# Two gate projections of group A moved from job 8 to the turn between groups B and A

## The chip, the cores and the metric

One core of one Trainium2 chip runs the whole program. The metric is device time in microseconds (us) of one launch, as the median of repeated runs. A core has five engines that run their own instruction streams in order and meet through semaphores: PE (TensorE, matmuls; its weight loads are listed as PEld), DVE (VectorE), ACT (ScalarE), POOL (GpSimd) and SP (SyncE, which here issues the DMAs).

## The reference, cut to what matters

One layer: `h = rms_norm(x)`, one projection of `h` (1024 tokens by 1024) onto 7,752 + 512 columns, four token mixers on slices of it, a SiLU gate on every mixer's output, one output projection and a residual.

```python
(aq, ak, av, ag, bq, bk, bv, bg, cq, ck, cv, cg, cf, d_in, dg) = _split(h @ w_in, IN_WIDTHS)
oa = rms_norm(differential_attention(rms_norm(aq), rms_norm(ak), av)) * (1 - lam_init)  # 4 heads
ob = rms_norm(stick_breaking_attention(bq, bk, bv))                                     # 8 heads
oc = rms_norm(forgetting_attention(rms_norm(cq), rms_norm(ck), cv, log_f))              # 8 heads
od = rwkv7_branch(d_in, ...)                                                            # 8 heads
mixed = concat([oa * silu(ag), ob * silu(bg), oc * silu(cg), od * silu(dg)])            # 2048 wide
out = x + mixed @ w_out
```

All gates are 16 blocks of 128 columns, numbered f = 0 to 15: 0 to 3 belong to A, 4 to 7 to B, 8 to 11 to C, 12 to 15 to D.

## The kernel before, in words

Everything is float32 in and out. A product is made of three fast matmuls on a high and a low part (`wh*hTh + wh*hTl + wl*hTh`), so one **projection** of 128 columns (`proj`, L271) is 2 halves of 512 tokens by 8 blocks of depth by 3 matmuls = 48 matmuls of 128x512, all on line L280, into two PSUM banks of the tag `pj`, of which there are only two. Its weights come in two pieces (`load_w`, L180): SP loads `raw` (256 KB, L186), ACT makes the high part `wh` (L191), POOL the low part `wl` (L192); each of these has two buffers, which one projection fills. After each half `evac` takes the bank out.

Order of work: the RWKV preparation of group D first; then 12 **jobs** (L1115), pairs of B heads (jobs 0 to 3), the A heads (4 to 7), pairs of C heads (8 to 11); then the RWKV chain, which begins once the normalised input and the weight buffers are given back after the last projection (`hp.close()`, L1150), and the output projection. In job i the program writes down the attention of job i, then the projections q, k, v of job i+1, then **fill**: the gate projections in `FILL[i]`. `FILL[8]` is gates 9, 0, 1. A planner turns this into one instruction order per engine: on its own estimate of time it takes on each engine the ready instruction that was written first. So fill and projections stand in the gaps of the attention that was written earlier, and buffers go to whoever was written earlier.

A gate is finished in one of two ways. Up to job 3 ACT's sigmoid table is loaded: `proj_gate` (L393) takes a sigmoid from the bank, multiplies on DVE, and stores 256 KB to `gates` in DRAM. From job 7 on the exp and ln tables are used: `proj_gate_exp` (L402) copies the bank to `gg` on ACT (L405), takes exp on ACT (L407), an add on DVE (L664), ln and exp on ACT (L665, L666), a multiply on POOL (L409), and stores (L410).

At the **turn** from B to A (job 3) the table is changed once (`exp_ln_tables`, L140/L141). The q and k of A's head 0 were projected before that and kept raw in DRAM (`late_qk`); after the table load they are loaded back (L365) and normalised half by half (`finish_qk`, L327: two squares on ACT, a difference on DVE, two `psn` matmuls, ln and exp on ACT, a product `qn` on DVE L339, then DMAs of line L133 that place q and k for the scores). The projections of A's head 1 follow.

After its attention every A head is stored raw (`otb`); `finish_later` loads it and its gate in a later job (`FIN`: gate 0 in job 8, gate 1 in job 9), normalises, multiplies and stores `mix`.

Tables of the file: `FILL` L45, `FIN` L46, `TMPB` L49 (buffers of the tag `tmp`), `HOLD` L55.

Of the kernel before, what the change touches and what calls it, by code (L numbers as in the profile page):

```python
# [10 lines left out]
F32 = mybir.dt.float32  # L11
# [3 lines left out]
AF = mybir.ActivationFunctionType  # L15
# [4 lines left out]
P = 128  # L20
S = 1024
DM = 1024
KT = DM // P
HS = 512
# [9 lines left out]
COL = dict(aq=0, ak=512, av=1024, ag=1536, bq=2048, bk=2560, bv=3072, bg=3584,  # L34
           cq=4096, ck=4608, cv=5120, cg=5632, cf=6144, dr=6152, dk=6664, dv=7176,
           dlo=7688, dg=7752)
# [6 lines left out]
EXP_LN_SET = 6  # L43
LATE_A = 4
FILL = {0: [4], 1: [5], 2: [6], 3: [7], 7: [8], 8: [9, 0, 1], 9: [10, 2], 10: [11, 3], 11: []}  # L45
FIN = {4: [4], 5: [5], 6: [6], 7: [7], 8: [0], 9: [1], 10: [2]}  # L46
OHW = 1152
NAV = 2
TMPB = 5  # L49
# [5 lines left out]
HOLD = (11,)  # L55
# [35 lines left out]
def hybrid_trunk_kernel(  # L91
# [23 lines left out]
    nc = tc.nc  # L115
# [3 lines left out]
    def pool(stack, name, bufs=1, space=None, side="left"):  # L119
        kw = {"side": side, "reuse_waits": "tile"} if space is None else {"space": space}  # L120
        return stack.enter_context(tc.tile_pool(name=name, bufs=bufs, **kw))

    dram = pool(ctx, "dram", 1, DRAM)
# [3 lines left out]
    def bank(tag, bufs, name):  # L127
        return psum.tile([P, HS], F32, tag=tag, bufs=bufs, name=name)
# [19 lines left out]
    def after(inst, first):  # L148
        tc.add_manual_dep(inst.ins, first.name if isinstance(first, mybir.InstLoadActFuncSet) else first.ins.name, mybir.DependencyInfo(
            mybir.DependencyClass.NoSync, mybir.DependencyReason.DATA), reason="order")  # L150
# [29 lines left out]
    def load_w(col, M=P, cols2=None):  # L180
        m1 = M if cols2 is None else M - cols2[1]
        wts = []
        for kh in range(2):
            rows = slice(kh * 4 * P, (kh + 1) * 4 * P)
            raw = wp.tile([P, 4, P], F32, tag="raw", bufs=2, name="raw")
            w_dma.append(nc.sync.dma_start(raw[:, :, :m1], w2[rows, col:col + m1].rearrange("(k p) c -> p k c", p=P)))  # L186
            if cols2 is not None:
                nc.sync.dma_start(raw[:, :, m1:M], w2[rows, cols2[0]:cols2[0] + cols2[1]].rearrange("(k p) c -> p k c", p=P))
            wh = wp.tile([P, 4, P], F32R, tag="wh", bufs=2, name="wh")
            wl = wp.tile([P, 4, P], F32R, tag="wl", bufs=2, name="wl")  # L190
            nc.scalar.copy(wh[:, :, :M], raw[:, :, :M])  # L191
            nc.gpsimd.tensor_sub(wl[:, :, :M], raw[:, :, :M], wh[:, :, :M].bitcast(F32))  # L192
            wts.append((wh, wl))
        return wts
# [48 lines left out]
    with xst:  # L243
# [14 lines left out]
        for hf in range(2):  # L258
            for kt in range(KT):
                ps = bank(("pj", "sc", "mm")[kt % 3] if hf == 0 else ("sc", "mm")[kt % 2], 2, "pst")  # L260
# [10 lines left out]
    def proj(col, evac, M=P, hold=None, wts=None):  # L271
        wts = load_w(col) if wts is None else wts
        pss = [bank("pj", 2, "pj") for _ in range(2)]
        for hf in range(2):
            cs = slice(hf * HS, (hf + 1) * HS)
            n = 0
            for kt in range(KT):
                wh, wl = wts[kt // 4]
                for a, b in ((wh, hTh), (wh, hTl), (wl, hTh)):
                    mm = nc.tensor.matmul(pss[hf][:M, :], lhsT=a[:, kt % 4, :M], rhs=b[:, kt, cs], start=n == 0, stop=n == 3 * KT - 1)  # L280
                    if n == 0 and hold is not None:
                        after(mm, hold)
                    n += 1
            evac(hf, cs, pss[hf])
# [5 lines left out]
    at = Att()  # L290
# [23 lines left out]
    def low_tiles(pl):  # L314
        at.units = 0
        at.low = [[], []]
        for h in range(2):
            other = slice(64 - 64 * h, 128 - 64 * h)
            for _ in range(3):
                t = pl.tile([P, HS], F32R, tag="ql", bufs=6, name=f"ql{h}")  # L320
                nc.gpsimd.memset(t[other].bitcast(F32), 0.0)
                at.low[h].append(t)
# [67 lines left out]
    gates = dram.tile([16, P, S], F32, name="gates")  # L390
    otb = dram.tile([8, P, S], F32, name="otb")

    def proj_gate(f, tmp):  # L393
# [5 lines left out]

        proj(COL["abcd"[f // 4] + "g"] + f % 4 * P, evac)  # L400

    def proj_gate_exp(f, hold=None):  # L402
        def evac(hf, cs, ps):
            g = at.cbp.tile([P, HS], F32, tag="gg", bufs=2, name="gg")
            nc.scalar.copy(g, ps)  # L405
            e = at.cbp.tile([P, HS], F32, tag="ge", bufs=2, name="gx")
            nc.scalar.activation(e, g, AF.Exp, scale=-1.0)  # L407
            sigmoid_of(e)
            nc.gpsimd.tensor_mul(e, g, e)  # L409
            nc.sync.dma_start(gates[f, :, cs], e)  # L410

        proj(COL["abcd"[f // 4] + "g"] + f % 4 * P, evac, hold=hold)

    def scores(t, h, qb, c0, c1, last=None):
        ps = bank("sc", 2, "sc")
# [247 lines left out]
    def sigmoid_of(e):  # L663
        nc.vector.tensor_scalar(e, e, 1e19, 1.0, op0=ALU.min, op1=ALU.add)  # L664
        nc.scalar.activation(e, e, AF.Ln)  # L665
        nc.scalar.activation(e, e, AF.Exp, scale=-1.0)  # L666
# [438 lines left out]
    with ExitStack() as st:  # L1105
        pl = pool(st, "attw", 1)
        low_tiles(pl)
        late_pools = st.enter_context(ExitStack())
        pp = pool(late_pools, "attp", 1)
        tmp = pool(late_pools, "attt", 1)  # L1110
        side = late_pools.enter_context(ExitStack())
        inv_load(pool(side, "ip", 1))
        bounds = INV_BOUNDS
        nxt = None
        for i, (pf, af, j) in enumerate(jobs):  # L1115
            cur = pf(j, pl, tmp) if nxt is None else nxt
            at.first = None
            af(j, cur, pl, pp, tmp)
            if i == 7:
                side.close()  # L1120
                at.cbp = pool(side, "cbp", 1)
            if i == 3:
                late = []
                nxt = proj_head_a(0, pl, tmp, late)
                for f in FILL[i]:
                    proj_gate(f, tmp)
                table = exp_ln_tables()
                for g in late:
                    g(table)
            else:  # L1130
                nxt = jobs[i + 1][0](jobs[i + 1][2], pl, tmp) if i + 1 < len(jobs) else None
            if i < 3:
                for f in FILL[i]:
                    proj_gate(f, tmp)
                gate_d(i, tmp)
                if i == 2:
                    gate_d(3, tmp)
            elif i >= 7:
                for f in FILL[i]:
                    proj_gate_exp(f, at.first if i in HOLD else None)  # L1140
            for f in FIN.get(i, []):
                for J in range(2):
                    finish_later(f, J, tmp)
            if i + 1 < len(bounds):
                with later(LATER):
                    inv_steps(bounds[i], bounds[i + 1], at.first)
                    if i + 2 == len(bounds):
                        inv_store()

        hp.close()  # L1150
        opr = pool(st, "opr", 1, side="right")
        rp = pool(st, "rp", 1, side="right")
        rwkv_chain_setup(rp)
        yts = {}

        def chain(c0, c1):
            for c in range(c0, c1):
                if c % 2 == 0:
                    yts[0] = rp.tile([P, 4, P], F32, tag="yt", bufs=2, name="yt")
                chunk_state(c, rp, yts[0], chunk_local(c + 1, rp) if c + 1 < NCH else iter(()))  # L1160
                if c % 2:
                    rwkv_norm(c // 2, yts[0], rp)

        for _ in chunk_local(0, rp):
            pass
        wo = {}
        chain(0, CUT1)
        split_w_early(pl, opr, wo)
        pair = out_blocks(0, 2, wo)
        for _ in range(EARLYG):  # L1170
            next(pair)
        chain(CUT1, CUT2)
        for h in at.held:
            finish(*h)
        for f in LASTF:
            for J in range(2):
                finish_later(f, J, tmp)
        late_pools.close()
        op = pool(st, "op", 1)
        if WFIRST:  # L1180
            split_w_late(op, opr, wo)
        chain(CUT2, NCH)
        if not WFIRST:
            split_w_late(op, opr, wo)
        for _ in pair:
            pass
        for tb in range(2, 8):
            for _ in out_blocks(tb, 1, wo):
                pass
# [29 lines left out]
```

## Time and profile before

| | us |
|---|---|
| median of 3 runs | 1552.37 (1550.95 to 1554.71) |
| the profiled execution | 1549.06 |
| its span, first to last instruction | 1546.9 |
| mean granted TensorE clock | 0.976 |
| busy: PE 94%, PEld 76%, DVE 66%, ACT 54%, POOL 52% | of the span |

The span leaves 2.16 us of the execution's own time outside. A busy PE is not a PE at its peak: matmuls overlap, one of 128x512 is listed with some 399 ns but the next can start after 0.23 us. A granted clock of 1.00 is 2.4 GHz; the other level is 1.2 GHz.

### The profile page before, as it was taken

How to read it: one execution, taken by the hardware profiler on the slowest of the kernel's cores; microseconds unless marked ns; L12 is line 12 of the kernel's file. 1: busy time of each engine (PE TensorE's matmuls, PEld its weight loads, DVE VectorE, ACT ScalarE, POOL GpSimd, SP SyncE). 2: the span in 40 equal slices, each digit the busy share in tenths (PEclk: the TensorE clock that was granted, in tenths of full speed). 3: DMA queues.
4: the chain of work that ended last, by engine and by line, in shares of the span. 5: the costliest groups of instructions: out<-in, count | busy, mean ns of one | idle time of the engine just before them, and what ended most of it. 6: DMA issues, size and time to landing. Idle time of an engine off the chain costs nothing.

```text
span 1546.9 us, 23668 instructions
## 1 busy us (share of the span) xinstructions
PE 1453.2 (94%) x8180; PEld 1180.9 (76%) x8180; DVE 1025.5 (66%) x1819; ACT 834.5 (54%) x1788; POOL 806.9 (52%) x869
## 2 busy tenths in 40 slices
PE   6899999999999998898998999989998898999999
PEld 4687878778888776676876778868777677888887
DVE  6666774497998887988888564464648766444321
ACT  6645554455656556656676676676766555111110
POOL 2455643756483832895967575656758654100000
PEclk9999999999999998798999999999999999999999
DMA  6545557322222323123234543243338557465231
GB/s 154 111 111 121 139 147 198 103 62 76 69 79 65 110 62 102 33 57 108 59 93 91 142 130 94 85 116 110 95 99 195 141 153 205 115 155 130 74 115 61
DMA packets 259759, 168.76 MB, mean 109 GB/s; under 512 B 127948, under 2 KB 222412, under 8 KB 259512
## 3 DMA queue, kind: packets, MB, share of 16 engines
q1 hardware_dynamic: 259640, 167.26, 40.6%
q8 instruction: 64, 1.05, 0.3%
q14 instruction: 55, 0.45, 0.1%
HBM read 107.40 MB, written 49.60 MB: 101 GB/s over the span
## 4 chain that ended last, share of the span: by engine, by line
PE 64%; DVE 12%; POOL 7%; issue 5%; DMA 5%; ACT 5%; SPq 2%; DVEq 0%; POOLq 0%; ACTq 0%
PE pj L280 31%; PE pso L956 10%; PE psf L993 5%; PE pt L439 4%; PE sc L419 2%; POOL yinv L881 2%; PE sc L423 2%; POOL ytmp L878 2%; PE po L449 2%; PE po L448 2%; DVE Pt L571 2%; POOL wl L192 1%; DMA k<-kl 1%; DMA raw<-in_w_in_dram 1%; DVE Pt L591 1%
## 5 line engine op out<-in xcount | busy, mean ns | idle before, releaser
L280 PE MATMUL pj<-hTh,wh 128*128 128x512 f32 (+1 forms) x1040 | 416.1, 400 | 9.9 <-DVE qn L339 4.2
L280 PE MATMUL pj<-hTh,wl 128*128 128x512 f32 (+1 forms) x1040 | 411.9, 399 | 8.9 <-POOL wl L192 6.2
L280 PE MATMUL pj<-hTl,wh 128*128 128x512 f32 (+1 forms) x1040 | 413.4, 398 | 1.6 <-DVE hTl L268 1.6
L192 POOL TENSOR_TENSOR wl<-raw,wh 128x512 fp32r<-128x512 f32 (+1 forms) x130 | 186.9, 1439 | 133.2 <-ACT wh L191 120.7
L280 PEld LDWEIGHTS pj<-hTh,wl 128*128 128x128 f32 (+1 forms) x1040 | 197.1, 190 | 56.1 <-POOL wl L192 12.9
L280 PEld LDWEIGHTS pj<-hTh,wh 128*128 128x128 f32 (+1 forms) x1040 | 197.9, 190 | 55.1 <-DVE qn L339 6.5
L280 PEld LDWEIGHTS pj<-hTl,wh 128*128 128x128 f32 (+1 forms) x1040 | 197.6, 190 | 41.8 <-DVE hTl L268 1.9
L442 ACT CAST pth<-pt 128x512 fp32r<-128x512 f32 x240 | 107.4, 481 | 84.9 <-PE pt L439 72.9
L443 DVE TENSOR_TENSOR ptl<-pt,pth 128x512 fp32r<-128x512 f32 x240 | 125.8, 551 | 36.3 <-ACT pth L442 35.2
L576 ACT ACTIVATE Pt<-Pt,st 128x512 f32<-128x512 f32 (+2 forms) x192 | 117.0, 613 | 46.2 <-DVE st L571 41.8
L419 PE MATMUL sc<-k,q 128*128 128x512 f32 (+3 forms) x288 | 114.3, 399 | 19.2 <-DVE st L571 13.6
L881 POOL TENSOR_TENSOR yinv<-yinv,ytmp 128x486 f32<-128x486 f32 (+44 forms) x106 | 123.5, 1165 | 5.8
L191 ACT CAST wh<-raw 128x512 fp32r<-128x512 f32 (+1 forms) x130 | 80.2, 617 | 85.9 <-PE pj L280 52.9
L498 DVE TENSOR_TENSOR_SCAN qs<-qs 128x128 f32<-128x128 f32 (+3 forms) x96 | 122.4, 1283 | 3.6 <-ACT qs L138 3.3
L439 PE MATMUL pt<-cst,Pt 128*128 128x128 f32 x720 | 118.6, 280 | 5.5 <-DVE ptl L443 2.1
L878 POOL TENSOR_TENSOR ytmp<-yinv 128x486 f32<-128x486 f32 (+44 forms) x106 | 109.3, 1031 | 4.8
L1086 POOL TENSOR_TENSOR yc<-yc,lbg 128x512 f32<-128x512 f32 x16 | 20.7, 1296 | 168.9 <-DVE yc L1080 168.2
L439 PEld LDWEIGHTS pt<-cst,Pt 128*128 128x128 f32 x720 | 87.9, 143 | 21.3 <-DVE Pt L591 3.8
L423 PE MATMUL sc<-k,ql 128*128 128x512 f32 (+3 forms) x288 | 103.0, 359 | 0.0
L956 PE MATMUL pso<-wol,omh 128*128 128x512 f32 x224 | 89.1, 398 | 0.0
L956 PE MATMUL pso<-woh,oml 128*128 128x512 f32 x224 | 88.7, 400 | 0.0
L956 PE MATMUL pso<-woh,omh 128*128 128x512 f32 x224 | 88.1, 396 | 0.0
(267 smaller groups left out, 3010.3 us busy)
## 6 DMA issues: line engine op xcount, KB each, us to landing
raw<-in_w_in_dram SPq DMA_DIRECT2D x128, 256.0 KB, 3.0
cb<-cum SPq DMA_DIRECT2D x16, 512.0 KB, 4.4
bd<-abky SPq DMA_DIRECT2D x32, 256.0 KB, 4.7
wraw<-in_w_out_dram SPq DMA_DIRECT2D x16, 512.0 KB, 4.6
om<-mix SPq DMA_DIRECT2D x32, 256.0 KB, 2.9
q<-q SPq DMA_DIRECT2D x48, 128.0 KB, 2.3
k<-kl SPq DMA_DIRECT2D x48, 128.0 KB, 2.4
gl<-gates SPq DMA_DIRECT2D x24, 256.0 KB, 3.3
```

What stands on the lines that cost most here:

```text
L192: nc.gpsimd.tensor_sub(wl[:, :, :M], raw[:, :, :M], wh[:, :, :M].bitcast(F32))
L280: mm = nc.tensor.matmul(pss[hf][:M, :], lhsT=a[:, kt % 4, :M], rhs=b[:, kt, cs], start=n == 0, stop=n == 3 * KT - 1)
L419: mm = nc.tensor.matmul(ps[:, :w], lhsT=t[f"q{h}"][qh][:, qs], rhs=t[f"k{h}"][:, c0:c1], start=True, stop=False)
L423: nc.tensor.matmul(ps[:, :w], lhsT=t[f"l{h}"][qh][:, qs], rhs=t[f"k{h}"][:, c0:c1], start=False, stop=not diag)
L439: nc.tensor.transpose(pt[:, (b - a) * P:(b - a + 1) * P], ptiles[b][kb // 4][:, kb % 4 * P:(kb % 4 + 1) * P], ident)
L442: nc.scalar.copy(ph[:, :n], pt[:, :n])
L443: nc.vector.tensor_sub(pl[:, :n], pt[:, :n], ph[:, :n].bitcast(F32))
L498: nc.vector.tensor_tensor_scan(q[:, :w][:, ::-1], q[:, :w][:, ::-1], q[:, :w][:, ::-1], 1.0 if after is None else after, op0=ALU.mult, op1 ...
L576: nc.scalar.activation(et[:, :w], et[:, :w], AF.Exp, scale=-1.0, bias=init, accum_out=st[:, 2 + i:3 + i])
L878: mul = nc.gpsimd.tensor_mul(t, y[:, a:a + n, r:r + 1].to_broadcast([P, n, r]), y[:, r:r + 1, :r].to_broadcast([P, n, r]))
L881: nc.gpsimd.tensor_add(y[:, a:a + n, :r], y[:, a:a + n, :r], t)
L956: mm = nc.tensor.matmul(ps[b][half], lhsT=l, rhs=r[half], start=n == 0, stop=n == 47)
```

## The change

Gates 0 and 1 are projected at the turn, after the table load has been written down and after head 0's late q and k. Their banks are copied to SBUF on DVE (tile `graw`, in the tag `tmp`) and stored raw in a new DRAM buffer `late_gates`. In job 8, in the place of the two projections, four loads bring the raw halves into `gg`, and the rest of the gate runs as before. The first matmul of each half carries an order after the table load (`hold`).

```diff
+TURN = (0, 1)
...
+    def gate_exp(f, cs, g):
+        e = at.cbp.tile([P, HS], F32, tag="ge", bufs=2, name="gx")
+        nc.scalar.activation(e, g, AF.Exp, scale=-1.0)
+        sigmoid_of(e)
+        nc.gpsimd.tensor_mul(e, g, e)
+        nc.sync.dma_start(gates[f, :, cs], e)
+
     def proj_gate_exp(f, hold=None):
         def evac(hf, cs, ps):
             g = at.cbp.tile([P, HS], F32, tag="gg", bufs=2, name="gg")
             nc.scalar.copy(g, ps)
-            e = at.cbp.tile([P, HS], F32, tag="ge", bufs=2, name="gx")
...
+            gate_exp(f, cs, g)
...
+    late_gates = dram.tile([len(TURN), P, S], F32, name="late_gates")
+
+    def proj_gate_raw(f, hold):
+        def evac(hf, cs, ps):
+            g = at.fin.tile([P, HS], F32, tag="tmp", bufs=TMPB, name="graw")
+            nc.vector.tensor_copy(g, ps)
+            nc.sync.dma_start(late_gates[TURN.index(f), :, cs], g)
+
+        proj(COL["abcd"[f // 4] + "g"] + f % 4 * P, evac, hold=hold)
+
+    def gate_from_raw(f):
+        for hf in range(2):
+            cs = slice(hf * HS, (hf + 1) * HS)
+            g = at.cbp.tile([P, HS], F32, tag="gg", bufs=2, name="gg")
+            nc.sync.dma_start(g, late_gates[TURN.index(f), :, cs])
+            gate_exp(f, cs, g)
...
                 for g in late:
                     g(table)
+                for f in TURN:
+                    proj_gate_raw(f, table)
...
                 for f in FILL[i]:
-                    proj_gate_exp(f, at.first if i in HOLD else None)
+                    if f in TURN:
+                        gate_from_raw(f)
+                    else:
+                        proj_gate_exp(f, at.first if i in HOLD else None)
```

## Rows read from the trace of the kernel before

**Rows 1.** The page: busy time by engine, and the granted clock in 40 slices.
```profile
PE 1453.2 (94%) x8180; PEld 1180.9 (76%) x8180; DVE 1025.5 (66%) x1819; ACT 834.5 (54%) x1788; POOL 806.9 (52%) x869
...
PEclk9999999999999998798999999999999999999999
```

**Rows 2.** Windows by stage: length, busy (instructions) of PE, PEld, DVE, ACT, POOL, clock, DMA.
```profile
581.00:594.00 13.00, 13.00 (x67) 10.58 (x67) 10.51 (x14) 7.35 (x15) 1.80 (x5) 1.00 0.14 42
...
597.00:617.40 20.40, 13.93 (x56) 9.90 (x54) 13.90 (x21) 13.80 (x28) 5.18 (x4) 0.75 0.52 152
617.40:641.00 23.60, 19.67 (x53) 13.40 (x54) 22.15 (x64) 17.64 (x47) 16.88 (x18) 0.57 0.14 39
641.00:860.00 219.00, 203.17 (x944) 163.02 (x944) 183.58 (x410) 142.68 (x335) 165.56 (x167) 0.95 0.34 85
884.00:938.60 54.60, 52.55 (x264) 43.38 (x262) 36.13 (x81) 42.27 (x95) 37.58 (x43) 1.00 0.41 121
938.60:984.30 45.70, 45.70 (x230) 38.15 (x229) 18.71 (x46) 28.91 (x61) 25.23 (x32) 1.00 0.29 87
984.30:1157.70 173.40, 167.33 (x814) 136.44 (x814) 94.40 (x223) 121.42 (x268) 111.61 (x130) 1.00 0.34 101
```

**Rows 3.** Chain of waits, 594 to 665 us: start, length, what; a late load.
```profile
598.07 5.12 DMA ql<-late_qk
```

**Rows 4.** Timeline of PE, job 10: start, length, instruction; dense projection.
```profile
1152.05 0.39 PE L280 MATMUL pj<-hTh,wl 128*128 128x512 f32 x1
1152.28 0.39 PE L280 MATMUL pj<-hTh,wh 128*128 128x512 f32 x1
```

**Rows 5.** Timeline of ACT, jobs 8 and 9: first weight casts, a gate's bank.
```profile
883.51 0.60 ACT L191 CAST wh<-raw 128x512 fp32r<-128x512 f32 x1
...
966.16 0.59 ACT L405 COPY gg<-pj 128x512 f32<-128x512 f32 x1 [3.74 <-PE pj L280]
...
984.33 0.62 ACT L191 CAST wh<-raw 128x512 fp32r<-128x512 f32 x1 [0.25 <-PE pj L280]
...
1065.94 0.62 ACT L191 CAST wh<-raw 128x512 fp32r<-128x512 f32 x1 [1.11 <-PE pj L280]
```

**Rows 6.** Groups of instructions by line, 938.6 to 984.3 us.
```profile
L191 ACT CAST wh<-raw 128x512 fp32r<-128x512 f32 x6 | 3.7, 616 | 4.8 <-issue 2.4 <-POOL gx L409 1.3 <-POOL wl L192 1.1
```

**Rows 7.** Timeline of ACT at the turn: table load, and A head 1's q bank.
```profile
593.60 1.28 ACT L141 ACT_TABLE_LOAD   x1
...
614.53 0.60 ACT L295 ACTIVATE qn<-pj 128x512 f32<-128x512 f32 x1
```

**Rows 8.** Timeline of PE at the turn.
```profile
596.09 0.39 PE L280 MATMUL pj<-hTh,wl 128*128 128x512 f32 x1
...
638.61 0.63 PE L280 MATMUL pj<-hTh,wh 128*128 128x512 f32 x1
639.03 0.63 PE L280 MATMUL pj<-hTl,wh 128*128 128x512 f32 x1
```

**Rows 9.** Timelines of DVE and SP at the turn: the freed bank, A head 1's k.
```profile
637.02 0.74 DVE L339 SCALAR_TENSOR_TENSOR qn<-pj,qkg,qn 128x512 f32<-128x512 f32 x1
...
661.04 1.11 SPq L133 DMA_DIRECT2D k<-kl  x2
```

**Rows 10.** By line, 597 to 641 us: transposes, normalisation's matmul, projection.
```profile
L439 PE MATMUL pt<-cst,Pt 128*128 128x128 f32 x36 | 8.4, 354 | 2.8 <-DVE ptl L443 2.1 <-DVE Pt L591 0.6
...
L298 PE MATMUL psn<-sqh,blkr 128*128 128x512 f32 x5 | 3.3, 665 | 1.4 <-ACT sqh L296 0.9 <-ACT qn L238 0.5
...
L280 PE MATMUL pj<-hTh,wh 128*128 128x512 f32 x2 | 1.3, 628 | 0.0
```

**Rows 11.** Tiles `ge` and `gg`: a DVE pass over a bank (ns min/median/max), ACT's waits.
```profile
L397 DVE TENSOR_TENSOR ge<-pj,ge x8: 676/683/692, 357.1 to 582.4; 128x512 f32<-128x512 f32 x8
...
  PE pj L280: 15.0, 8
```

**Rows 12.** The page's DMA issues: count, KB each, us to landing.
```profile
gl<-gates SPq DMA_DIRECT2D x24, 256.0 KB, 3.3
```

More of the change, by code (lines that the diff above doesn't have):

```diff
@@ L405, in evac @@
             nc.scalar.copy(g, ps)
-            e = at.cbp.tile([P, HS], F32, tag="ge", bufs=2, name="gx")
[L407 to L410, printed above, removed]
-        proj(COL["abcd"[f // 4] + "g"] + f % 4 * P, evac, hold=hold)
+            gate_exp(f, cs, g)
+        proj(COL["abcd"[f // 4] + "g"] + f % 4 * P, evac, hold=hold)
+    late_gates = dram.tile([len(TURN), P, S], F32, name="late_gates")
[11 more added lines that the diff above has]
+            gate_exp(f, cs, g)
     def scores(t, h, qb, c0, c1, last=None):
```

## The prediction

> **What bounds the kernel now.** The page first: PE is busy for 94% of the span [rows 1], so work taken off PE counts only where PE has no gap, and work put on it costs only where it has none. The granted clock tells the two apart: full nearly everywhere, with a dent in slices 16 to 19 [rows 1]. Windows by stage then show both places of this change [rows 2]. From 938.6 to 984.3, where job 8's gates 9, 0 and 1 are projected, PE is busy for all of the 45.7 us while DVE has 18.7, ACT 28.9 and POOL 25.2: PE sets the pace. At the turn it is otherwise. From 597 to 641 us PE is listed busy for 33.6 of 44.0 us with only 109 matmuls, at a granted clock of 0.75 and 0.57; the 45.7 us of job 8 hold 230 at 1.00. The chain of waits there runs through the late q and k of A's head 0, for example 5.12 us for one load [rows 3], and from 617.4 on DVE is the full engine, 22.15 of 23.6 us [rows 2].
>
> Why does PE not take the next projections into that gap? The timelines answer. The q projection of A's head 1 was done early, its last matmul at 596.09, before and under the tail of job 3 [rows 2, 8]. Its two halves fill both `pj` banks, and ACT begins to square the first only at 614.53, behind head 0's late work [rows 7]. The bank comes free with `qn` at 637.02 [rows 9], and the k projection starts at 638.61 [rows 8]. So the gap is a wait for banks, and it matters: head 1's k is sent at 661.04 [rows 9], and its scores need it.
>
> **What job 8 loses.** Two projections are 96 matmuls. Dense ones start 0.23 us apart (1152.05, 1152.28; 0.227 over a longer run) [rows 4], so PE loses 96 x 0.227 = 21.8 us. Four copies on ACT (0.59 us) [rows 5] and four casts (0.62) [rows 6] go too, 4.8 us. Would something else take over? The fill of job 8 lasts from 883.51 to 984.33, 100.8 us [rows 5]; without the 21.8 it is 79.0. ACT is busy for 42.3 + 28.9 = 71.2 us of about that stretch [rows 2], less 4.8 is 66.4; POOL has 62.8, DVE 54.8. PE stays the longest, but ACT follows closely. After 984.3, where a job has five projections and not six, PE is idle for 6.1 of 173.4 us, 3.5% [rows 2]; the same share of 79 us is 2.8. I take 21.8 - 2.8 = 19.0 us. The ends: 21.8, and 10.9 if the attention's own chain keeps one of the two back. A sign for the upper end is that job 9, with one projection less, needs 1065.94 - 984.33 = 81.6 us [rows 5], 19.2 less for one.
>
> What job 8 gains is four loads of 256 KB; like ones land in 3.3 us [rows 12]. They depend on nothing in job 8 but a free `gg` and can be sent long before use, so I price them at nothing: cover is the PE-paced stretch itself. Without it each would hold ACT for 3.3 us, 13 in all, as much as ACT has to spare (79.0 - 66.4 = 12.6). Later stages begin when the last projection is done, so I let the 19.0 go through to the end.
>
> **What the turn gains.** The projections ask for weights before head 1's q does, so they take the two weight buffers that q has now (its first cast is among ACT's work before the table load), and wait for the load, which ends at 593.60 + 1.28 = 594.9 [rows 7]. So q's 48 matmuls, 10.9 us that now lie before 597, come after: 144 matmuls, 32.7 us, follow the load. The tail of job 3 gains little by losing them: DVE is busy for 10.5 of 13.0 us there [rows 2]; between 0 and 2.5 us, and I take 0, DVE being nearly full.
>
> Room for them, at full clock: the 109 matmuls of 597 to 641, without six of head 1's k (three groups of two), are 36 transposes and 67 others. The transposes were busy for 8.4 us at the low clock [rows 10], 4.2 at the high one; the others take at most 67 x 0.227 = 15.2. That leaves 44.0 - 19.4 = 24.6, and 2.1 from 594.9 to 597: 26.7 us. Head 1's q would end 6.0 us past 641, at 647.0, and k start there and not at 638.6: 8.4 us late. Six of k's matmuls ran 0.42 us apart (638.61, 639.03) [rows 8] and now take 0.23, 1.2 us back. I take a slip of 7 us. Nothing hides it: head 1's scores follow its k at once. From 641 to 860 PE is idle for 15.8 of 219 us [rows 2], so some might be made up, but I keep the 7. The ends: -3 (no slip, and a faster chain, see below) and +21.8 (the whole added PE time).
>
> Beside PE: four copies out of PSUM on DVE. No such copy is in the trace; the nearest, a product with one operand in the bank, takes 0.68 us [rows 11], so 2.7 us. From 597 to 617.4 DVE is idle for 6.5 us [rows 2]: nothing, and 2.7 if they fall after 617.4. Four more casts on ACT and subtractions on POOL at the turn, four loads and four stores on SP: ACT is idle for 6.6 us before 617.4 and POOL for 15 [rows 2]; SP's extra transfers meet the late loads, 5.12 us at worst now [rows 3]. Each is between 0 and some 3 us, and the slip holds them.
>
> **Sum.** 1549.06 - 19.0 + 7 = 1537 us for the profiled execution. The median of before is 3.3 us above it, so 1540 us.
>
> **Rivals.**
> *The full clock shortens the turn itself.* With fill PE would not pause, and the late chain's matmuls would run at 2.4 GHz, not 1.2: the ten `psn` matmuls, 665 ns each now [rows 10] against some 0.4, give back 2.5 us, and if that and the earlier banks also remove the slip, the sum is -19.0 - 2.5 = -21.5, 1531 us. For it: 0.57 and 1.00 in the windows. Against: the chain is mostly DMA, ACT and DVE. Beside it stands the Trainium skill, "TensorE: Matmul & The Clock Gate", Part 1: "the default state is throttled, and activity releases the throttle." By that rule filling the gap would raise the clock; the trace agrees, with 0.57 in the sparse window and 1.00 in the dense one.
>
> *The raw projections miss the gap.* If head 1's q still goes first, both banks stay locked until 637 and the 96 matmuls run in A's heads: +21.8 - 19.0 = +2.8, 1555 us; with a part in the gap, less. For it: the order is the planner's by its own time, which the trace does not show. Against: the weights are asked for in the order of writing. This is also the case where the change does not do what it says.
>
> *Slower: DVE stands at the copies.* DVE works in order, and a copy placed too early holds what is behind it: the differences and `qn` of the late chain, then the first softmax blocks. ACT waited so for gate banks, 15.0 us over 8 of 16 [rows 11], at most 3.74 [rows 5]. Four waits of 3.74 are 15.0; with 2.7 for the copies and the slip of 7, 24.7 against 19.0: +5.7, 1558 us. It decides from 22 us of waits, copies and slip on. The Trainium skill lists ScalarE's and VectorE's queues as strict FIFO (the same page, its opening table); the trace agrees in that ACT's 3.74 us passed with nothing else started.
>
> **How the numbers follow.** The forecast has 0.50, for 1532 to 1546 (gain 15 to 21.8, slip 3 to 12); the full clock 0.18; the missed gap 0.15, a third of it still faster by over 0.2% and the rest within; DVE 0.17. A measurement of this kernel tells some 0.2%, 3.1 us, from no change. Faster 0.50 + 0.18 + 0.05 = 0.73, the same 0.10, slower 0.17. The unknown ends are -21.8 - 3 = -25 and -10.9 + 24.5 = +14; a range from 1528 to 1557 leaves out about 0.15, nearly all above.
>
> **What would show it.** Right: 96 of 128x512 projection matmuls more between 594.9 and 641 with the clock near 1.00; head 1's k projection starting 3 to 12 us later than 638.6 counted from the table load; the fill from job 8's to job 9's first q cast down from 100.8 to about 82 us, PE still without gaps there. Wrong: k's projection over 15 us late, DVE idle before `graw` for more than 10 us, or the fill of job 8 at 90 us with ACT full. Then the sum ends near no change or above it.

## The result, and the profile after

The changed kernel takes 1529.96 us (median of 4 runs, 1526.44 to 1530.86), the kernel before 1553.26 (1550.95 to 1554.71) beside it: a ratio of 0.9851, 95% interval [0.9832, 0.9869], or 20 to 26 us less. The forecast was 1540. The profiled execution took 1530.82 us, with a span of 1529.0.

The page of the changed kernel, to be held against [rows 1]:

```profile
PE 1446.8 (95%) x8180; PEld 1179.0 (77%) x8180; DVE 1018.2 (67%) x1823; ACT 829.2 (54%) x1784; POOL 803.1 (53%) x869
...
PEclk9999999999999999999999999999989999999999
```

PE has the same 8180 matmuls as before, so no work is gone: the projections were moved. Of the 17.9 us by which the span is shorter, 11.5 are PE time listed as idle and 6.4 PE time listed as busy (1453.2 and 1446.8), the latter for the same matmuls at a mean granted clock of 0.983 and not 0.976. The Trainium skill ("Perfetto Trace Analysis", section "Identifying the Most-Contended Engine") says that matmul busy time is not a good measure of how close a kernel is to its roofline, since matmuls are pipelined. The trace agrees: before, PE was listed idle for only 10.4 us between 597 and 641 us [rows 2], and that stretch now holds 59 matmuls more. The dent of the clock in slices 16 to 19 is gone, though the shorter windows below still show 0.85 and 0.92. Windows by stage (columns as in [rows 2]) show the turn and job 8:

```profile
581.00:594.00 13.00, 12.01 (x61) 9.30 (x60) 12.70 (x19) 11.10 (x24) 2.54 (x5) 1.00 0.27 82
...
597.00:620.20 23.20, 17.48 (x76) 12.58 (x74) 13.41 (x19) 13.64 (x27) 8.66 (x7) 0.85 0.49 136
620.20:641.00 20.80, 20.77 (x92) 17.37 (x93) 13.76 (x38) 7.97 (x21) 13.76 (x15) 0.92 0.38 115
...
885.70:956.70 71.00, 68.49 (x339) 56.53 (x338) 38.32 (x89) 48.50 (x108) 41.11 (x50) 1.00 0.36 101
956.70:1040.50 83.80, 81.20 (x390) 66.88 (x389) 48.93 (x110) 64.24 (x140) 58.97 (x69) 0.98 0.43 126
```

From 597 to 641 us the two windows now hold 168 matmuls of PE where they held 109 [rows 2], at a clock of 0.85 and 0.92 where it was 0.75 and 0.57. Line 281 alone, the projections, in 594 to 641 us (columns: PE, PEld, clock, DMA), first before, then after:

```profile
594.00:641.00 47.00, 4.81 (x16) 3.75 (x16) 0.68 0.31 87
```

```profile
594.00:641.00 47.00, 26.12 (x105) 19.74 (x105) 0.89 0.41 118
```

So 89 projection matmuls more fell into that stretch: the gap took the gates. The timelines of PE, ACT, DVE and SP at the turn of the changed kernel (start, length, instruction, and in brackets the wait ahead of it):

```profile
591.33 0.39 PE L281 MATMUL pj<-hTh,wh 128*128 128x512 f32 x1
...
608.58 0.63 PE L281 MATMUL pj<-hTh,wl 128*128 128x512 f32 x1
...
624.02 0.53 PE L281 MATMUL pj<-hTh,wh 128*128 128x512 f32 x1
...
648.98 0.39 PE L281 MATMUL pj<-hTh,wl 128*128 128x512 f32 x1
...
655.11 0.50 PE L281 MATMUL pj<-hTh,wh 128*128 128x512 f32 x1
...
593.97 1.28 ACT L142 ACT_TABLE_LOAD   x1
...
644.61 0.60 ACT L296 ACTIVATE qn<-pj 128x512 f32<-128x512 f32 x1 [1.66 <-PE pj L281]
...
623.07 1.28 DVE L423 COPY graw<-pj 128x512 f32<-128x512 f32 x2
630.31 0.68 DVE L423 COPY graw<-pj 128x512 f32<-128x512 f32 x1
635.25 0.69 DVE L423 COPY graw<-pj 128x512 f32<-128x512 f32 x1 [4.25 <-PE pj L281]
...
654.32 0.73 DVE L340 SCALAR_TENSOR_TENSOR qn<-pj,qkg,qn 128x512 f32<-128x512 f32 x1
...
675.84 1.11 SPq L134 DMA_DIRECT2D k<-kl  x2
```

Read against [rows 7], [rows 8] and [rows 9]: gate 0's first matmul stands ahead of the table load (the `hold` sets a place in the order, not a wait); head 1's q is squared at 644.61 and not 614.53; its bank comes free at 654.32, not 637.02; its k projection starts at 655.11, not 638.61; its k is sent at 675.84, not 661.04. Locally the head is 15 to 17 us late. DVE stands once at a copy, for 4.25 us. The other way round the wait is longer: gate 0's last matmul starts at 608.58, its two banks are copied only at 623.07, and gate 1's first matmul follows at 624.02, so for 15.4 us PE runs no projection. DVE was busy for 13.4 of 23.2 us up to 620.2, so what kept the copies was their place in DVE's order and not a full DVE. Head 1's q then runs to 648.98, and its k waits for q's banks until 655.11.

Job 8's and job 9's first weight casts on ACT, against [rows 5]:

```profile
885.74 0.61 ACT L192 CAST wh<-raw 128x512 fp32r<-128x512 f32 x1
...
956.68 0.62 ACT L192 CAST wh<-raw 128x512 fp32r<-128x512 f32 x1
...
1040.48 0.61 ACT L192 CAST wh<-raw 128x512 fp32r<-128x512 f32 x1
```

The fill of job 8 shrank from 100.8 to 70.9 us. That is 8 more than the 96 matmuls' 21.8, because a fill's length counts whatever else falls between two casts: about 206 other matmuls before (264 + 230 [rows 2], less 288 of projections), 140 now (339, less 199 of line 281). It is therefore no measure of the gain. The whole run after the first change is, and the next views cut it in two: line 280 or 281 alone, in the **A part** (from the store of job 3's first output block to ACT's last output of head A3, 0.6 to 2 us ahead of its store) and the **C part** (from there to the end). First before, then after:

```profile
577.20:898.70 321.50, 176.31 (x661) 127.65 (x661) 0.92 0.33 88
898.70:1546.90 648.20, 184.20 (x739) 135.81 (x739) 0.99 0.44 122
```

```profile
581.40:909.20 327.80, 197.31 (x774) 144.56 (x774) 0.97 0.35 92
909.20:1529.00 619.80, 158.59 (x626) 115.97 (x626) 0.99 0.47 128
```

Ahead of that store PE, DVE, ACT and POOL run the same instructions in the same order, and this execution came there 4.2 us later by chance; from there on it is 969.7 against 947.6, 22.1 less, close to the medians. The A part did 113 projection matmuls more, 25.7 us of PE at 0.227, and grew by only 6.3. The C part did 113 fewer, and shrank by 28.4. Of the 113, 96 are the gates; 17 were due later anyway. All lines of the A part (columns as in [rows 2]), before and after, tell where the other 19.4 us were found:

```profile
577.20:898.70 321.50, 292.83 (x1333) 232.82 (x1332) 254.36 (x566) 211.50 (x490) 216.07 (x230) 0.92 0.33 88
```

```profile
581.40:909.20 327.80, 306.25 (x1460) 245.94 (x1458) 252.79 (x578) 216.32 (x503) 223.66 (x239) 0.97 0.35 92
```

PE's listed idle time went from 28.7 to 21.6 us, 7.1 less. Its listed busy time grew by only 13.4 us for 127 more matmuls, at a granted clock of 0.97 and not 0.92: some 51 us at the low level became some 20 (twice the missing share, the low level being half of the full). So the room was part idle time and part, an estimated 12 us (25.7 - 13.4), time listed as busy in which matmuls had run at the low clock or too far apart to overlap.

### The profile page after: what moved, and what is told of

Same layout as the page of the kernel before. It is cut to its first block, busy times and chain, and to the rows that moved or that the text cites. A ratio compares the mean times of both kernels' runs of the same rounds, so it can differ in the third digit from the quotient of the medians.

```text
span 1529.0 us, 23670 instructions
## 1 busy us (share of the span) xinstructions
PE 1446.8 (95%) x8180; PEld 1179.0 (77%) x8180; DVE 1018.2 (67%) x1823; ACT 829.2 (54%) x1784; POOL 803.1 (53%) x869
## 4 chain that ended last, share of the span: by engine, by line
PE 63%; DVE 14%; POOL 7%; ACT 6%; issue 5%; DMA 4%; SPq 1%; DVEq 0%; POOLq 0%; ACTq 0%
PE pj L281 30%; PE pso L977 10%; PE psf L1014 5%; PE pt L460 3%; PE sc L440 2%; PE sc L444 2%; DVE qs L519 2%; POOL yinv L902 2%; PE po L470 2%; PE po L469 2%; POOL ytmp L899 1%; DVE Pt L521 1%; DMA raw<-in_w_in_dram 1%; DVE Pt L592 1%; DVE ptl L464 1%
```

## Experiments

Edits are against the changed kernel unless said. Each run stands beside runs of the kernel before on the same chip, whose medians were 1550.7 to 1552.2 us.

**One side of the move alone.** `e1_drop` doesn't project gates 0 and 1 at all (job 8 loads other data); `e2_both` projects them twice, at the turn and in job 8.

```diff
 e1_drop
-            nc.sync.dma_start(g, late_gates[TURN.index(f), :, cs])
+            nc.sync.dma_start(g, raws[TURN.index(f), :, cs])
...
-                for f in TURN:
-                    proj_gate_raw(f, table)
...
 e2_both
-                    if f in TURN:
-                        gate_from_raw(f)
-                    else:
-                        proj_gate_exp(f, at.first if i in HOLD else None)
+                    proj_gate_exp(f, at.first if i in HOLD else None)
```

> The changed kernel (1530 us) without the two raw projections at the turn; job 8 finishes gates 0 and 1 from other raw data of the same size, so the output's part of these two gates is not the reference's. Theory (the two projections stand in time in which PE waited, at the turn and in A's heads): 1523 to 1531 us, at most 7 us faster than the changed kernel. Rival 1 (PE sets the pace there too, and the gain comes from ACT's and POOL's work and waits that left job 8): 1508 to 1512 us, the whole 21.8 us faster. Rival 2 (what helps is that A head 1's q no longer takes both banks before the table load): here q goes first again, so slower than the changed kernel, about 1534 us.

> The kernel before (1553 us) with two more projections: raw gates 0 and 1 at the turn, stored and never read, and job 8 as before. Theory (time in which PE waited takes them): 1553 to 1560 us. Rival 1 (PE paced at the turn): about 1575 us, 21.8 more. Rival 2 (q behind the table load is what helps, and the projections cost nothing beside): about 1546 to 1551 us, faster than before.

Measured: e1_drop 1530.97 us, 0.9865 [0.9847, 0.9883]; e2_both 1551.83, 1.0005 [0.9994, 1.0015]. The four kernels make a square. With no gates at the turn, job 8's two projections are worth 1.35%, 21 us; with gates at the turn 1551.83 - 1529.96 = 21.9, or 23.9 by the ratios. The turn's two cost -0.9 to +2.3 us (e2's interval), and about nothing beside job 8 without them (1530.97 and 1529.96). e1_drop fits its theory; e2_both lies between its theory, 1.2 us below it, and rival 2, 0.8 above it, and its ratio is that of no change. e1_drop also bears on the clock: it has job 8's gain at a mean granted clock of 0.977, near the 0.976 of before, so that gain needs no higher clock. The two parts, first of e1_drop, then of e2_both:

```profile
578.80:898.80 320.00, 175.07 (x661) 126.30 (x661) 0.94 0.33 89
898.80:1527.50 628.70, 163.65 (x643) 119.51 (x643) 0.99 0.46 125
```

```profile
578.80:906.80 328.00, 197.29 (x774) 144.51 (x774) 0.97 0.35 92
906.80:1547.10 640.30, 181.25 (x722) 133.07 (x722) 0.99 0.46 123
```

The A part is the same in e2_both as after (328.0 and 327.8, 774 projections in both), and the same in e1_drop as before. So the square compares like with like. And it shows where the slip went: in e2_both the A part is 6.5 us longer than before and the C part 7.9 shorter, with 17 projections fewer to do (739 against 722, 3.9 us); the other 4.0 us were not traced.

**One gate, and three.** `TURN = (0,)`, and `TURN = (0, 1, 9)` with DVE and with ACT copying the banks; `e5_drop3` leaves the three projections out altogether.

```diff
-TURN = (0, 1)
+TURN = (0,)          # e3_one
+TURN = (0, 1, 9)     # e4_three, e5_drop3, e11_three_act
...
-            nc.vector.tensor_copy(g, ps)
+            nc.scalar.copy(g, ps)      # e11_three_act
...
-                for f in TURN:
-                    proj_gate_raw(f, table)      # e5_drop3, which loads raws as e1_drop does
```

> The change for gate 0 alone; gate 1 is projected in job 8. Theory (each projection gives PE 10.9 us in job 8 and takes idle time at the turn): half the gain, 1540 to 1543 us. Rival 1: as before or slightly faster, over 1545 us. Rival 2 (the gain comes with the first raw projection, which pushes q behind the load): most of the gain already, 1530 to 1536 us.

> The change for gates 0, 1 and 9. Theory: idle time at the turn was about 31 us by start-to-start gaps of PE and is half full now, A's heads have more, so the third brings less than the first two: 1520 to 1528 us, 2 to 10 us faster than the changed kernel. If the turn is full with two: 1530 to 1535 us, the third costs in A's heads what it saves in job 8. Rival 1 and 2: no gain from a third, 1530 us or more.

> The kernel with gates 0, 1 and 9 moved (1545 us), without its three raw projections at the turn; job 8 finishes the three gates from other raw data, so these gates' part of the output is not the reference's. Theory A (the third projection costs at the turn and in A's heads, about 25 us, while job 8 still gives some 10 for it): 1518 to 1523 us. Theory B (job 8 has nothing more to give, since without fill its attention sets the pace): 1529 to 1534 us or more, near the kernel with two dropped (1531).

> Three gates (0, 1 and 9) projected raw at the turn, as in the run that took 1544.8 us, but with the banks copied out by ScalarE; nothing is left out. The copy's engine alone changed the time little with two gates (1530.0 against 1533.3). Theory A (the third has no room in the gap and costs some 15 us there, whatever the order): 1540 to 1549 us. Theory B (the 15 us were stalls of that one recorded order in the A heads, which a small change of the order takes away, as between the two kernels without the hold, 1554.6 and 1535.7): 1526 to 1536 us.

Measured: one gate 1540.89 us, 0.9927 [0.9911, 0.9942], half the gain. Three: 1544.77, 0.9956 [0.9941, 0.9971], and 1554.87 with ACT's copies, 1.0015 [0.9998, 1.0031]: the third gate loses 15 to 25 us. That is a miss of e4_three's theory, and e11_three_act lies above both of its theories. None of the three at all: 1528.56, 0.9845 [0.983, 0.9861], nearest to theory B. So a third gate left out gives only 2.4 us more than two (1530.97 against 1528.56), which the intervals don't tell from nothing, and three at the turn cost 16 to 26 (1544.77 and 1554.87 against 1528.56), of which the first two cost about nothing. All lines of e1_drop and then of e5_drop3, from A3's end to the last projection (columns as in [rows 2]):

```profile
898.80:1121.90 223.10, 218.74 (x1072) 180.93 (x1071) 137.56 (x304) 166.61 (x364) 150.88 (x175) 0.99 0.38 111
```

```profile
907.30:1129.50 222.20, 211.45 (x1021) 173.31 (x1020) 128.74 (x300) 160.87 (x354) 145.22 (x171) 0.98 0.37 107
```

51 matmuls fewer in nearly the same time, 0.9 us less: PE is listed busy for 95% there, no longer for 98%. So PE no longer sets the pace; that the heads' own chain of waits does, with the projections as its fill, is the likely reading, and no single wait was traced. Nor is the 2.4 us this stretch alone: e5_drop3's A part is 7.6 us longer than e1_drop's (327.6 and 320.0) with the same projections, and its end after the last projection 8.1 us shorter (397.5 and 405.6) with the same matmuls. And the two parts of e4_three, then of e11_three_act:

```profile
579.20:923.50 344.30, 201.74 (x779) 149.19 (x780) 0.96 0.33 89
923.50:1542.90 619.40, 159.72 (x622) 115.72 (x620) 0.99 0.48 129
```

```profile
577.10:933.30 356.20, 218.97 (x848) 158.31 (x848) 0.97 0.36 97
933.30:1551.10 617.80, 143.10 (x552) 104.84 (x552) 0.98 0.45 122
```

The two lose it differently. e4_three pushes other projections out of the A part (779, only 5 more than after) and is 16.5 us longer there. e11_three_act does 74 more than after there (16.8 us) in 28.4 us more, and its C part, with 74 fewer, is only 2.0 us shorter.

**Another place.** The two raw projections in job 4, with both copy engines; and gate 9 raw in job 5, beside two at the turn.

```diff
-                for f in TURN:
-                    proj_gate_raw(f, table)
...
+            if i == 4:                       # e6_job4, e12_job4_act (with nc.scalar.copy)
+                for f in TURN:
+                    proj_gate_raw(f, None)
...
-                for f in TURN:
+                for f in TURN[:2]:           # e8_third_job5, TURN = (0, 1, 9)
...
+            if i == 5:                       # e8_third_job5
+                proj_gate_raw(9, None)
```

> The change with its two raw projections written down in job 4 (after A head 1's q, k, v) and not at the turn; the order after the table load is not needed there. Theory (the turn's gap is what takes them without cost): the gap stays empty, A's heads take them at a price of 5 to 20 us, 1536 to 1550 us. Rival (idle time anywhere in A's heads takes them): 1529 to 1533 us, as the change.

> The two raw gates projected in job 4 in place of the turn, as in the run that took 1561.8 us, but with the banks copied out by ScalarE; nothing is left out. Theory A (inside A's heads the 96 matmuls find no gap, so they cost at least their own 21.8 us): 1549 to 1562 us. Theory B (most of the 31 us were stalls of that one recorded order): 1530 to 1542 us.

> Gates 0 and 1 raw at the turn and gate 9 raw in job 5, after A head 2's q, k, v. If A's heads still have room for one projection and job 8 still gives some 10 us for it: 1520 to 1527 us, a better version. If A's heads charge for it what job 8 saves: 1528 to 1534 us. If job 8 has nothing to give: 1531 to 1545 us.

Measured: 1561.8 us, 1.0059 [1.0047, 1.0072], and 1558.99 with ACT's copies, 1.0064 [1.0038, 1.0089]; for e8_third_job5 1537.72, 0.9922 [0.99, 0.9944]. Put one job later, the same two projections cost 28 to 31 us (against e1_drop) where they cost none at the turn, above the highest that was expected of e6_job4 and within e12_job4_act's theory A. The two parts of e6_job4:

```profile
577.60:916.60 339.00, 190.93 (x731) 138.36 (x732) 0.94 0.33 87
916.60:1557.00 640.40, 171.84 (x670) 124.04 (x669) 0.98 0.46 125
```

Against e1_drop the A part does 70 more projections, 15.9 us at 0.227, in 19.0 us more; the C part 27 more, 6.1 us, in 11.7 more. In job 4 the work finds no gap (PE's listed idle time in the A part is 31.7 us, 30.3 in e1_drop) and pays its full price; the 8.7 us beyond that weren't traced to one wait. And 1537.72 for e8_third_job5, 7.8 above after, is near a projection's full 10.9 us less the 2.4 that a third gate gives in job 8.

**The order and the copy.** `e7_nohold` lets the gates go without the order after the table load; `e9_actcopy` copies the banks on ACT; `e10_nohold_act` does both.

```diff
-            nc.vector.tensor_copy(g, ps)
+            nc.scalar.copy(g, ps)            # e9_actcopy, e10_nohold_act
...
-                    proj_gate_raw(f, table)
+                    proj_gate_raw(f, None)   # e7_nohold, e10_nohold_act
```

> The change without the order after the table load, so that gate 0's projection may run under the tail of job 3, as A head 1's q did before. Theory (the turn takes two projections without cost, so a third projection's time more gives nothing): 1527 to 1533 us, as the change. Rival (the change loses because PE has nothing to fill job 3's tail with): 1519 to 1526 us. Rival (without PE's fill the tail of job 3 ends sooner, 3.8 us in the profile of the change, and that is part of its gain): 1533 to 1536 us.

> The kernel after, but the raw gate banks of the turn are copied out by ScalarE in place of VectorE (line 423); nothing is left out. In the kernel after, VectorE stood 4.25 us at the copy of gate 1's last bank and copied gate 0's two banks only at 623. Theory A (what the turn does to the A heads doesn't reach the end, so neither wait costs anything): 1527 to 1533 us. Theory B (the banks are freed too late, and head 1's k behind them moves earlier with them): 1518 to 1526. Theory C (ScalarE, which carries the casts of q, k and of the weights at that place, is the scarcer engine there, and the first softmax pieces come later): 1534 to 1542.

> The kernel without the hold on the raw projections (line 1152: None in place of the table load), and with the banks copied out by ScalarE in place of VectorE; nothing is left out. Without the hold alone it was 1554.6 us: gate 0 was projected ahead of the table load, and its two banks were then copied by VectorE only at 614, with TensorE idle from 597 on. Theory A (the late copy is the cause: VectorE's queue holds the banks): with ScalarE they are free before 602 us, and the time is 1528 to 1536. Theory B (the cause is the place in TensorE's order, gate 1 in front of head 0's late k and first scores, and a table load that nothing then covers): 1548 to 1556 again, with TensorE at under 0.75 of full clock between the table load and 620 us.

Measured: e7_nohold 1554.57 us, 1.0018 [1.0005, 1.003], above all three of its expectations; e9_actcopy 1533.29, 0.9879 [0.9855, 0.9902], between theories A and C; e10_nohold_act 1535.65, 0.9891 [0.9863, 0.992]. e9_actcopy's copies came no sooner than DVE's: its table load starts at 591.21 and the first copy at 620.16, 28.9 us later, against 29.1 after. So what banks freed early would give at the turn was not tested. After e7_nohold I took DVE's late copy (614 us, with no projection on PE from 596.6 to 614.9) for the cause. e10_nohold_act was to free the banks before 602 us; the tile's view shows that it didn't (copies, ns min/median/max, first and last start):

```profile
L423 ACT COPY graw<-pj x4: 579/583/592, 616.9 to 629.3; 128x512 f32<-128x512 f32 x4
```

The banks were held even longer, to 616.9, and yet the time is that of theory A. So the bank isn't the cause of the 18.9 us between the two. Nor is the place of gate 1, which theory B named: in both kernels its 48 matmuls stand ahead of head 0's first scores, which come at 626.22 in e7_nohold and later still, at 628.76, in e10_nohold_act. Neither mechanism holds. The parts of e7_nohold, then of e10_nohold_act:

```profile
577.30:930.60 353.30, 212.60 (x821) 154.90 (x821) 0.97 0.34 90
930.60:1548.80 618.20, 146.28 (x579) 108.07 (x579) 0.98 0.46 125
```

```profile
579.00:916.40 337.40, 209.07 (x819) 152.18 (x819) 0.97 0.35 94
916.40:1527.30 610.90, 147.05 (x581) 108.24 (x581) 0.99 0.46 127
```

Nearly the same projections in each part, and 15.9 and 7.3 us more of stalls. (The profiled execution of e10_nohold_act took 1529.14 us, 6.5 less than its median.) Which of e7_nohold's waits makes them is open. One was seen, ACT standing 6.6 us at a load of `otl` in head A3, but e9_actcopy has one of 4.9 us at the same load and ends at 1533. The hold is worth 2.4 us with ACT's copies and 24.6 with DVE's; I can't call it a price of the hold.

No version beats the change: e9_actcopy's and e10_nohold_act's intervals overlap with its own, and e1_drop and e5_drop3 leave work out.

## Why the prediction was right, and which step failed

The direction and the place were right, and the time fell inside the outer range of 1528 to 1557, but 2 us below the forecast's own 1532 to 1546. The sum's two errors, a gain 2.8 us too small and a slip of 7 us that was not seen at the end, go the same way, so none hid the other. By its steps:

**Job 8: 19.0 us forecast, 21 to 24 measured.** PE does set the pace there. The 2.8 us taken off for new idle time did not come; e1_drop and e2_both, with 21 us and 21.9 us, give the full 96 x 0.227 = 21.8. The four projections that job 8 keeps are still enough to hold PE at 98% over the C heads (e1_drop); three are not (95%, e5_drop3).

**The four loads: nothing, with 13 us without cover.** The tile's view of `gg` in the changed kernel names one wait of ACT, 1.4 us, out of four loads that land in 3.3 to 3.6 us:

```profile
  DMA gg<-late_gates: 1.4, 1
```

**The tail of job 3: taken as 0.** No run changes it alone. The table load came 12.6 us after the store of job 3's first block, 16.4 before (593.97 - 581.4, 593.60 - 577.2), so 3.8 us were gained, more than the 0 to 2.5; in e1_drop, e7_nohold and e10_nohold_act, where a whole projection stands ahead of the load again, it is 16.4 too. But the gates' first matmuls were in the tail too, which the prediction excluded: it took the order after the load for a wait.

**The slip of 7 us kept to the end: this is the step that failed, and the sum's error is there.** It was two statements. The first, that head 1's k comes 7 us late, was too small: the k projection starts 16.1 us later, counted from the table load (16.5 less 0.4), past the 15 us that the prediction itself had named as a sign of being wrong. The working had q end at 647.0 "and k start there". q's end came out nearly so, its last matmul at 648.98, though gate 1 had waited for gate 0's banks until 624.02. But k could not start there: q's two halves fill both banks, as the prediction had found for the kernel before, and the first came free with DVE's `qn` at 654.32. That wait of 6.1 us is a term that the working left out. The second, that nothing hides it, was wrong by more: the end did not move with head 1's k. Counted from job 3's first store, k is 12.3 us late, by A3's end only 6.3 us were left, and by the end of the run none: e2_both, which has the whole slip and none of job 8's gain, runs in the time of before. What the end followed here is how much of PE's time was filled, and not the lateness of one tile: the A part did 25.7 us of projections more in 6.3 us more, and the 17 projections done early came off the C part. A price of the slip by itself, without the filling that comes with it, no run isolates.

**DVE's copies: 2.7 us, hidden.** Measured 2.65 (1.28 + 0.68 + 0.69), with one wait of 4.25. e9_actcopy takes both off DVE and gains nothing, so DVE's own time at them was not on the path. That a copy could come late and keep PE's projections waiting, 15.4 us here, the prediction did not ask; what that costs is open.

**Sum.** With 21.8 in place of 19.0, and a turn of about nothing in place of 7, 1549.06 - 21.8 = 1527 us for the profiled execution, and 1531 on the scale of the medians; measured 1529.96.

**The rivals.** *Full clock* gave 1531, which is close in number, but not by its mechanism: it needed the slip gone, and the slip doubled; and e2_both leaves the turn 0.9 us of gain at most, not 2.5. The clock did rise, as the denser windows show. What the higher clock alone is worth can't be told apart here: it comes with the matmuls that fill the gap, and the 12 us of the A part are an estimate of room in which it has only a share. *Raw projections miss the gap* fell at the turn, with 89 of 96 matmuls more in the stretch; e6_job4 shows that it would have been worse than priced, +0.6% and not +0.2%. *DVE stands at the copies* fell: 4.25 us, not 15, and off the path. Of the prediction's own signs of being right, 89 matmuls more (of 96) came, at a clock of 0.85 and 0.92, and the late k missed.

## What to carry to other kernels

Where one engine is near full, count a moved piece of work by the time of that engine that it fills and leaves, stage by stage, and not by how late a tile becomes; a head that was 16 us late did not move the end here, since the engine had other work meanwhile. A gap has a size: two projections went into this one for nothing, a third made the kernel 15 to 25 us slower, and two in a stage without a gap cost 28 to 31. And the stage that gives work away needs some of it as fill: the first two were worth 10.9 us each, the third 2.4, which is within the noise. The count has a limit: the losses of e4_three and e7_nohold came with the same work of PE, as stalls that it did not foresee.

## What the runs showed that I had not expected

An order between two instructions that only the scheduler sees is not a wait on the chip: gate 0's matmuls ran 2.6 us ahead of the table load that they were ordered after (591.33 and 593.97).

How far a small change of a recorded order reaches: two kernels that differ only in the engine of four copies of 0.58 to 0.69 us (e7_nohold, e10_nohold_act) are 18.9 us apart, with PE doing nearly the same projections in both parts, while the same edit beside the hold (after, e9_actcopy) moves the time by some 3 us. A single variant of this kernel can thus be off by more than 1% for reasons that I could not trace. The conclusions above rest on the square and on pairs that agree in sign (e4_three and e11_three_act, e6_job4 and e12_job4_act); e7_nohold, whose pair disagrees, is left open, and e8_third_job5 has none.
